# A second scatter table for one token tile, and both tables added when they are loaded

## The chip, the cores and the metric

The kernel runs on one core of one Trainium2 chip. The metric is device microseconds (us) of one execution.

## The reference

One layer of a residual block over 1024 tokens of width 1024: two groups of attention heads, an output projection, and then a PEER channel mixer, which is the part that matters here. For each token, 8 retrieval heads pick 16 of 16384 experts each (product keys of 128 x 128), so a token has 128 experts, each with a gate:

```python
u = expert_down[eb]
act = jax.nn.gelu(jnp.einsum('td,thkd->thk', xb, u), approximate=False) * gb
vv = expert_up[eb]
return jnp.einsum('thk,thkd->td', act, vv)
```

`eb` are the indices of the chosen experts, `gb` their gates. All is float32.

## The kernel before, in words

Tokens lie in eight tiles of 128. Five tiles (block A, tiles 0 to 4) take the dense way through the mixer: every expert is computed for every token, and the activation is multiplied by a gate table, which is zero wherever an expert was not chosen. The three others (block B) take the sparse way: each token's experts are gathered row by row.

The front (to about 1190 us) is the attention, the projections and the routing of both blocks. TensorE, VectorE and ScalarE are fed there by several program streams that a Python merge interleaves (`mrg`), and a planner in the framework sets the order on each queue by priority and its own timing model. The gate tables are made in the front, in two ways:

- Tiles 1 to 4: `gbuild` makes them with one-hot matrices and matmuls, and writes them to the DRAM tensor `gd` (16 DMAs of 2 MB on SP's queue, L1079).
- The one remaining tile (`NSC` is 1): its table `gds[0]` in DRAM, of 128 x 16384 floats (8.4 MB), is first filled with zeros by `zero` (L433 to L438: 16 DMAs of 512 KB from the zero tile `zt`, on SP's queue, pinned in program order, one for each 0.5 of the stream's progress). Then `scatter` (L1028 to L1038) issues 128 indirect DMAs on GpSimd (POOL), one for each of head and choice. Each adds 128 gates, one per token, into the table at computed addresses. A scatter reads and writes the table that the one before wrote, so the framework lets each wait for the landing of the one before.

The indices and gates of the scatters come from `cands` in five groups (L1020 writes the indices). From about 625 us to the end of the front the scatters are all that GpSimd does.

The dense loop (`for gi in range(NG)`, L1368) runs over 32 groups of four chunks; a chunk is 128 experts. The order on TensorE, VectorE and ScalarE is written out by hand there. For each chunk, `split_d` and `split_u` split the weights into a high and a low part (VectorE makes the low part, L1288, L1296), `gelu_s` computes the scores and the GELU (L379 to L381, ScalarE L1304), `mul_g` multiplies by the gates on VectorE (L1310 for the scattered tile, L1312 for the four others), and `split_c` splits the product. After four chunks `up` multiplies by the up weights into ten PSUM banks (L1327 to L1329). `loadg` loads the gates of a group of four chunks: on GpSimd's queue for the first two groups, on SP's queue behind and ahead of the weight loads (L1267, L1269) for the others. `mul_g` of a group's first chunk needs them:

```python
gg, g4 = k.g
c = k.i1 % CG
g3 = k.ge[:, :NSC * P].rearrange("p (s t) -> p s t", t=P)
V.tensor_mul(g3, g3, gg[:, :, c, :])
```

Between the steps of the dense loop, `sp_` (`pump`) issues steps of the sparse way: first the last three `cands` groups of block B, then per expert slot an indirect gather on GpSimd into a ring of five buffers (L1218 for the down rows, L1231 for the up rows) and one VectorE instruction (L1220, L1236).

Of the kernel before, what the change touches and what calls it, by code (L numbers as in the profile page):

```python
# [11 lines left out]
F32 = mybir.dt.float32  # L12
F32R = mybir.dt.float32r
# [4 lines left out]
OP = mybir.AluOpType  # L18
AX = mybir.AxisListType.X

P = 128
# [13 lines left out]
NE = 128  # L35
NSLOT = 128
EPS = 1e-6
BIG = 1e30
# [3 lines left out]
CG = 4  # L42
NG = NE // CG
NPT = 4
NSC = ND - NPT
# [60 lines left out]
def tile_kernel(ctx: ExitStack, tc: tile.TileContext, x, ccol, w_ada, badac, bgt2, gcols, w_in, w_f, bf_, gout,  # L106
                w_out, w_q, keysT, edown, eup, wdense, gfin, out, dbg=None, stop=None):
    nc = tc.nc
    V, S, G, PE = nc.vector, nc.scalar, nc.gpsimd, nc.tensor
    dma = nc.sync.dma_start  # L110
    dbg = dbg or {}

    cst = ctx.enter_context(tc.tile_pool(name="cst", bufs=1))
    dram = ctx.enter_context(tc.tile_pool(name="dram", bufs=1, space=bass.MemoryType.DRAM))

    identf = cst.tile([P, P], F32, name="identf")
    make_identity(nc, identf)
    identr = cst.tile([P, P], F32R, name="identr")
    V.tensor_copy(identr, identf)
    onesf = cst.tile([P, P], F32, name="onesf")  # L120
    V.memset(onesf, 1.0)
    zf = cst.tile([P, 1], F32, name="zf")
    V.memset(zf, 0.0)
    zt = cst.tile([P, P], F32, name="zt")
    V.memset(zt, 0.0)
    mfox = cst.tile([P, P], F32R, name="mfox")
    G.affine_select(mfox, zt, pattern=[[-1, P]], compare_op=OP.is_ge, fill=BIG, base=0, channel_multiplier=1)
    msb = cst.tile([P, P], F32R, name="msb")
    G.affine_select(msb, zt, pattern=[[-1, P]], compare_op=OP.is_gt, fill=-BIG, base=0, channel_multiplier=1)
    iof = cst.tile([P, P], F32, name="iof")  # L130
    G.iota(iof, [[1, P]], base=0, channel_multiplier=0, allow_small_or_imprecise_dtypes=True)
    mhalf = cst.tile([P, 8], F32, name="mhalf")
# [22 lines left out]
    vsp = dram.tile([8, P, T], F32, name="vsp")  # L155
    wsp = dram.tile([24, 2, P, D], F32R, name="wsp")
    gd = dram.tile([NPT * P // SB, P, NE * SB], F32, name="gd")
    gds = [dram.tile([NE * P * P, 1], F32, name="gds%d" % i) for i in range(NSC)]
    pidx = cst.tile([P, 1], F32, name="pidx")
    G.iota(pidx, [[0, 1]], base=0, channel_multiplier=1, allow_small_or_imprecise_dtypes=True)  # L160

# [34 lines left out]
    hpa = ctx.enter_context(tc.tile_pool(name="hpa", bufs=2))  # L196
    hp_[0] = hpa
    wp = front.enter_context(tc.tile_pool(name="wp", bufs=2))
    ps = front.enter_context(tc.tile_pool(name="ps", bufs=2, space=bass.MemoryType.PSUM))
    pin = tc.keep_in_program_order  # L200

# [728 lines left out]
    def cands(blk, gi, v16, i16):  # L930
# [94 lines left out]
            V.tensor_copy(blk.e[:, cols], tm)  # L1025
        yield 1

    def scatter(b, gi):  # L1028
        for k in range(16):
            for r in range(8):  # L1030
                i = (8 * gi + r) % b.nt
                if i < NSC:
                    c_ = (8 * gi + r) * 16 + k
                    off = bass.IndirectOffsetOnAxis(ap=b.e[:, c_:c_ + 1], axis=0)
                    with tc.high_priority(offset=min(0, tc.cur_priority - LOWP)):
                        G.indirect_dma_start(out=gds[i], out_offset=off, in_=b.g[:, c_:c_ + 1], in_offset=None,  # L1036
                                             compute_op=OP.add)
                    yield 1  # L1038

# [134 lines left out]
    def tpool(name, **kw):  # L1174
        return ctx.enter_context(tc.tile_pool(name=name, bufs=2, reuse_waits="tile", **kw))

    dps = tpool("dps", space=bass.MemoryType.PSUM)
    dp0, dpw, dp3, dp2, dp = [tpool(n_) for n_ in ("dp0", "dpw", "dp3", "dp2", "dp")]
# [64 lines left out]
    def pump(n):  # L1243
        while n > 0 and bgs:
            if next(bgs[0], 0) == 0:
                bgs.pop(0)
            else:
                n -= 1
# [23 lines left out]
    def loadg(gi):  # L1272
        i1 = gi * CG
        dma = nc.sync.dma_start if gi > 1 else G.dma_start
        gg = dp.tile([P, NSC, CG, P], F32, name="gg", tag="gg", bufs=2)
        for k in range(NSC):
            dma(gg[:, k], gds[k].rearrange("(p c t) o -> p c (t o)", p=P, t=P)[:, i1:i1 + CG])
        g4 = dp.tile([P, NPT * P // SB, CG, SB], F32, name="g4", tag="g4", bufs=2)
        dma(g4, gd[:, :, i1 * SB:(i1 + CG) * SB].rearrange("s p (c t) -> p s c t", t=SB))
        return gg, g4  # L1280

    def split_d(k, act):
        if act:
            k.dh = dp3.tile([P, D], F32R, name="dh", tag="dh", bufs=2)
            S.activation(k.dh, k.wfd, AF.Copy)
        else:
            k.dl = dp3.tile([P, D], F32R, name="dl", tag="dl", bufs=2)
            V.tensor_sub(k.dl, k.wfd, k.dh.bitcast(F32))  # L1288

    def split_u(k, act):  # L1290
        if act:
            k.uh = dp2.tile([P, D], F32R, name="uh", tag="uh", bufs=UB)
            S.activation(k.uh, k.wfu, AF.Copy)  # L1293
        else:
            k.ul = dp2.tile([P, D], F32R, name="ul", tag="ul", bufs=UB)
            V.tensor_sub(k.ul, k.wfu, k.uh.bitcast(F32))  # L1296

    def gelu_s(k):
        k.ge = dp0.tile([P, TD], F32, name="ge", tag="ge", bufs=2)
        for h in range(2):  # L1300
            cs = slice(h * TH, (h + 1) * TH)
            sp = dps.tile([P, HT], F32, name="sp", tag="sp", bufs=2)
            mm3(sp[:, :TH], k.dh, k.dl, hh, hl, cs)
            S.activation(k.ge[:, cs], sp[:, :TH], AF.Gelu)  # L1304

    def mul_g(k):
        gg, g4 = k.g
        c = k.i1 % CG
        g3 = k.ge[:, :NSC * P].rearrange("p (s t) -> p s t", t=P)
        V.tensor_mul(g3, g3, gg[:, :, c, :])  # L1310
        g3 = k.ge[:, NSC * P:].rearrange("p (s t) -> p s t", t=SB)
        V.tensor_mul(g3, g3, g4[:, :, c, :])  # L1312

    def split_c(k, act):
        if act:
            k.ch = dp2.tile([P, TD], F32R, name="ch", tag="ch", bufs=CG)
            S.activation(k.ch, k.ge, AF.Copy)
        else:
            k.cl = dp2.tile([P, TD], F32R, name="cl", tag="cl", bufs=CG)
            V.tensor_sub(k.cl, k.ge, k.ch.bitcast(F32))  # L1320

    def up(gi, bk, po, k, c):
        tb, dhf = divmod(bk, 2)
        tcs = slice(tb * P, (tb + 1) * P)
        ds_ = slice(dhf * HT, (dhf + 1) * HT)
        per = bk in pers
        PE.matmul(po, k.ch[:, tcs], k.ul[:, ds_], start=c == 0 and (gi == 0 or not per), stop=False)  # L1327
        PE.matmul(po, k.ch[:, tcs], k.uh[:, ds_], start=False, stop=False)  # L1328
        PE.matmul(po, k.cl[:, tcs], k.uh[:, ds_], start=False, stop=c == CG - 1 and (gi == NG - 1 or not per))  # L1329
# [20 lines left out]
    def sp_(n):  # L1350
        pump(n)
# [4 lines left out]
    def nextload():  # L1356
        i1 = next(loads, None)
        if i1 is not None:
            ready.append(load(i1))
# [7 lines left out]
    gcur = loadg(0)  # L1367
    for gi in range(NG):  # L1368
        grp = []
        gnext = loadg(gi + 1) if gi + 1 < NG else None  # L1370
        prev = None
        for c in range(CG + 1):
            cur = nxt if c < CG else None
            if c < CG:
                cur.g = gcur
                grp.append(cur)
            nxt = ready.pop(0) if c < CG and ready else nxt
            if c < CG - 1 and not hasattr(nxt, "dh"):
                split_d(nxt, True)
            if c == CG and gi + 1 < NG:  # L1380
                split_d(nxt, True)
            if cur is not None:
                split_u(cur, True)
            if prev is not None:
                mul_g(prev)
                split_c(prev, True)
            if c < CG - 1 and not hasattr(nxt, "dl"):
                split_d(nxt, False)
            if prev is not None:
                sp_(1)  # L1390
                split_c(prev, False)
            if cur is not None:
                gelu_s(cur)
                split_u(cur, False)
                nextload()
                sp_(PUMP_C - (prev is not None))
            prev = cur
        pos = {}
        for c0, c1 in ((0, CG - 1), (CG - 1, CG)):
            for bk in order[:NPERS]:  # L1400
                for c in range(c0, c1):
                    up(gi, bk, pers[bk], grp[c], c)
        sp_(PUMP_U)
        if gi + 1 == NG:
            pump(10000)
            gf = gfin_tile(dp3, "dh", 2, dma)
            dense_done(order[:NPERS], gf)
        if gi + 1 < NG:
            split_d(nxt, False)
        for n, bk in enumerate(order[NPERS:]):  # L1410
            po = dps.tile([P, HT], F32, name="po", tag="po", bufs=6 - NPERS)
            for c in range(CG):
                up(gi, bk, po, grp[c], c)
            evac(gi, bk, po)
            if gi + 1 < NG and PD and n in (PD, PD + 1) and ready:
                split_d(ready[0], n == PD)
            if gi + 1 == NG:
                dense_done([bk], gf)
            sp_(PUMP_V)
        gcur = gnext  # L1420
# [47 lines left out]
```

## Time and profile before

| | us |
|---|---|
| median of 3 runs (range) | 3099.52 (3094.88 to 3106.32) |
| the profiled execution | 3094.74 |
| its span | 3093.0 |
| TensorE busy in the span | 2871.2 (93%) |
| VectorE busy | 2569.4 (83%) |
| GpSimd busy | 1398.6 (45%) |

The span is the time from the first to the last instruction of the profiled execution; 1.7 us lie around it. Shares of busy time are means over stages with different limits, so the stages are read one by one. Matmuls overlap, so a busy TensorE is not a TensorE at its peak.

### The profile page before, as it was taken

The page shows a single profiled execution, that of the slowest core. Times are in us where ns is not written, and L with a number is a line of the kernel's source. Part 1 is how long each engine was busy: PE and PEld are TensorE (multiplying, and loading weights), DVE is VectorE, ACT ScalarE, POOL GpSimd, SP SyncE. Part 2 cuts the span into 40 slices and gives each one's busy share as a digit, 9 for nine tenths or more (in the row PEclk, how much of TensorE's full clock was granted, in tenths as well). Part 3 has the DMA queues.
Part 4 walks back from the last instruction along what each step waited for, and adds up shares of the span by engine and source line. Part 5 has one row for each costly group of instructions (what it writes and reads, how often), then busy time and mean ns, then how long its engine had stood idle before and what let it go on. Part 6 is the DMA issues. An engine that isn't in the chain of part 4 may idle for free.

```text
span 3093.0 us, 47927 instructions
## 1 busy us (share of the span) xinstructions
PE 2871.2 (93%) x17472; PEld 2657.2 (86%) x17472; DVE 2569.4 (83%) x5250; ACT 1187.6 (38%) x2148; POOL 1398.6 (45%) x962
## 2 busy tenths in 40 slices
PE   5899998998989895489999999999999999999997
PEld 4898998987879895479999899899998988989986
DVE  7676655899997886488889898898898988989996
ACT  5566655446776952132213222122231221322212
POOL 0000000033343423136666776666677656657771
PEclk9999999999999998789999999999999999999998
DMA  7996455655426674359999999999999999999994
GB/s 261 292 305 195 138 224 183 208 172 172 140 45 228 248 260 137 92 206 342 352 339 344 345 336 337 352 351 349 328 343 343 342 331 342 359 328 340 344 331 182
DMA packets 347196, 840.14 MB, mean 272 GB/s; under 512 B 48184, under 2 KB 155728, under 8 KB 344912
## 3 DMA queue, kind: packets, MB, share of 16 engines
q1 hardware_dynamic: 215072, 423.83, 39.9%
q0 software_dynamic: 131888, 413.26, 37.9%
q8 instruction: 137, 2.24, 0.3%
q14 instruction: 99, 0.81, 0.1%
HBM read 734.11 MB, written 102.86 MB: 271 GB/s over the span
## 4 chain that ended last, share of the span: by engine, by line
PE 52%; DVE 22%; DMA 11%; issue 7%; ACT 4%; POOL 3%; SPq 0%; DVEq 0%; POOLq 0%; ACTq 0%
PE sp L379 7%; PE sp L381 6%; PE sp L380 6%; DMA ring<-in_eup,e 5%; PE po L1327 3%; PE po L1328 3%; PE po L1329 3%; DVE sacc L1236 3%; PE pers L1327 2%; PE pers L1328 2%; PE pers L1329 2%; PE proj L379 2%; PE tp L1074 2%; POOL ring L1231 2%; PE proj L380 2%
## 5 line engine op out<-in xcount | busy, mean ns | idle before, releaser
L379 PE MATMUL sp<-hT,dl 128*128 128x320 f32 x2048 | 636.7, 311 | 75.3 <-ACT ge L1304 66.2
L1231 POOL DMA_INDIRECT ring<-in_eup,e x384 | 587.8, 1531 | 249.2 <-DVE sacc L1236 127.7
L1218 POOL DMA_INDIRECT ring<-in_edown,e x384 | 513.5, 1337 | 386.6 <-DVE ring L1220 157.8
L380 PE MATMUL sp<-hT,dh 128*128 128x320 f32 x2048 | 635.9, 311 | 0.0
L381 PE MATMUL sp<-hT,dh 128*128 128x320 f32 x2048 | 635.9, 310 | 0.0
L1236 DVE SCALAR_TENSOR_TENSOR sacc<-ring,sdot,sacc 128x1024 f32<-128x1024 f32 x381 | 488.4, 1282 | 61.9 <-DMA ring<-in_eup,e 56.6
L1220 DVE SCALAR_TENSOR_TENSOR ring<-ring,sx 128x1024 f32<-128x1024 f32 x384 | 461.3, 1219 | 75.5 <-DMA ring<-in_edown,e 73.5
L1036 POOL DMA_INDIRECT gds<-g,e x128 | 247.5, 1933 | 524.1 <-DMA gds<-g,e 370.8
L379 PEld LDWEIGHTS sp<-hT,dl 128*128 128x128 f32 x2048 | 387.5, 189 | 77.4 <-ACT ge L1304 67.6
L1293 ACT ACTIVATE uh<-wfu 128x1024 fp32r<-128x1024 f32 x128 | 134.8, 1053 | 677.6 <-PE po L1329 677.6
L380 PEld LDWEIGHTS sp<-hT,dh 128*128 128x128 f32 x2048 | 387.6, 189 | 1.2
L381 PEld LDWEIGHTS sp<-hT,dh 128*128 128x128 f32 x2048 | 387.3, 189 | 0.0
L1327 PE MATMUL po<-ul,ch 128*128 128x512 f32 x768 | 304.0, 396 | 19.0 <-DVE accB L1336 11.1
L1328 PE MATMUL po<-uh,ch 128*128 128x512 f32 x768 | 301.0, 392 | 0.0
L1329 PE MATMUL po<-uh,cl 128*128 128x512 f32 x768 | 300.6, 391 | 0.0
L1304 ACT ACTIVATE ge<-sp 128x320 f32<-128x320 f32 x256 | 110.6, 433 | 490.6 <-PE sp L381 470.0
L1328 PE MATMUL pers<-uh,ch 128*128 128x512 f32 x512 | 199.6, 390 | 0.0
L1327 PE MATMUL pers<-ul,ch 128*128 128x512 f32 x512 | 199.5, 390 | 0.0
L1329 PE MATMUL pers<-uh,cl 128*128 128x512 f32 x512 | 199.2, 389 | 0.0
L1327 PEld LDWEIGHTS po<-ul,ch 128*128 128x128 f32 x768 | 145.3, 189 | 58.0 <-DVE accB L1336 19.9
L303 POOL TENSOR_TENSOR i<-ms,mhalf 128x4 f32<-128x4 f32 (+1 forms) x16 | 22.1, 1380 | 333.8 <-DVE ms L301 333.8
L1329 PEld LDWEIGHTS po<-uh,cl 128*128 128x128 f32 x768 | 145.3, 189 | 30.9
(306 smaller groups left out, 6469.3 us busy)
## 6 DMA issues: line engine op xcount, KB each, us to landing
wfd<-in_wdense SPq DMA_DIRECT2D x128, 512.0 KB
wfu<-in_wdense SPq DMA_DIRECT2D x128, 512.0 KB
gd<-gt SPq DMA_DIRECT2D x16, 2048.0 KB
g<-gd SPq DMA_DIRECT2D x30, 1024.0 KB
wa<-in_w_ada SPq DMA_DIRECT2D x96, 256.0 KB
wf<-in_w_in SPq DMA_DIRECT2D x48, 512.0 KB
wsp<-wh SPq DMA_DIRECT2D x24, 512.0 KB
wsp<-wl SPq DMA_DIRECT2D x24, 512.0 KB
```

The source lines that it names most:

```text
L379: PE.matmul(pt, wl[:, c], hh[:, kd, cs], start=kd == 0, stop=False)
L380: PE.matmul(pt, wh[:, c], hl[:, kd, cs], start=False, stop=False)
L381: PE.matmul(pt, wh[:, c], hh[:, kd, cs], start=False, stop=kd == KD - 1)
L1036: G.indirect_dma_start(out=gds[i], out_offset=off, in_=b.g[:, c_:c_ + 1], in_offset=None, compute_op=OP.add)
L1218: G.indirect_dma_start(out=r, out_offset=None, in_=edown, in_offset=bass.IndirectOffsetOnAxis(ap=bs.e[:, c_:c_ + 1], axis=0))
L1220: (V.scalar_tensor_tensor(r, r, 1.0, sx, op0=OP.mult, op1=OP.mult, accum_out=s_[:, j:j + 1]))
L1231: G.indirect_dma_start(out=r, out_offset=None, in_=eup, in_offset=bass.IndirectOffsetOnAxis(ap=bs.e[:, c_:c_ + 1], axis=0))
L1236: (V.scalar_tensor_tensor(acc, r, s_[:, j:j + 1], acc, op0=OP.mult, op1=OP.add))
L1293: S.activation(k.uh, k.wfu, AF.Copy)
L1327: PE.matmul(po, k.ch[:, tcs], k.ul[:, ds_], start=c == 0 and (gi == 0 or not per), stop=False)
L1328: PE.matmul(po, k.ch[:, tcs], k.uh[:, ds_], start=False, stop=False)
L1329: PE.matmul(po, k.cl[:, tcs], k.uh[:, ds_], start=False, stop=c == CG - 1 and (gi == NG - 1 or not per))
```

## The change

There are two DRAM tables for the scattered tile instead of one. `zero` fills both (32 DMAs of 512 KB), and the scatters go to the two in turn. `loadg` loads the group's piece of both, the second into a new tile `gg2` with a single buffer, and the first `mul_g` of a group adds the two on VectorE (128 x 512 floats). `loadg` of the next group is no longer issued at the start of a group, but after the `mul_g` of the group's first chunk. To make room for `gg2`, four small constant tiles (`identr`, `zt`, `mfox`, `msb`, 2 KB per partition in all) move into a pool of the front that is freed before the dense loop; the instructions that fill them come later in the program by that.

```diff
-    gds = [dram.tile([NE * P * P, 1], F32, name="gds%d" % i) for i in range(NSC)]
+    gds = [dram.tile([NE * P * P, 1], F32, name="gds%d" % i) for i in range(2)]
...
+    nsct = [0]
...
                 if i < NSC:
+                    nsct[0] ^= 1
...
-                        G.indirect_dma_start(out=gds[i], out_offset=off, in_=b.g[:, c_:c_ + 1], in_offset=None,
+                        G.indirect_dma_start(out=gds[nsct[0]], out_offset=off, in_=b.g[:, c_:c_ + 1], in_offset=None,
                                              compute_op=OP.add)
...
-        gg = dp.tile([P, NSC, CG, P], F32, name="gg", tag="gg", bufs=2)
-        for k in range(NSC):
-            dma(gg[:, k], gds[k].rearrange("(p c t) o -> p c (t o)", p=P, t=P)[:, i1:i1 + CG])
+        gg = dp.tile([P, CG, P], F32, name="gg", tag="gg", bufs=2)
+        g2 = dp.tile([P, CG, P], F32, name="gg2", tag="gg2", bufs=1)
+        for k in range(2):
+            dma((gg, g2)[k], gds[k].rearrange("(p c t) o -> p c (t o)", p=P, t=P)[:, i1:i1 + CG])
...
-        g3 = k.ge[:, :NSC * P].rearrange("p (s t) -> p s t", t=P)
-        V.tensor_mul(g3, g3, gg[:, :, c, :])
+        if c == 0:
+            V.tensor_add(gg, gg, g2)
+        g3 = k.ge[:, :NSC * P]
+        V.tensor_mul(g3, g3, gg[:, c, :])
...
-        gnext = loadg(gi + 1) if gi + 1 < NG else None
+        gnext = None
...
                 mul_g(prev)
+                if c == 1 and gi + 1 < NG:
+                    gnext = loadg(gi + 1)
```

## Rows read from the trace of the kernel before

**Rows 1.** The page's 40 slices: GpSimd (POOL), busy tenths.
```profile
POOL 0000000033343423136666776666677656657771
```

**Rows 2.** Busy us (x instructions) by stretch; clock, DMA share, GB/s.
```profile
core 0: us, PE busy (x) PEld busy (x) DVE busy (x) ACT busy (x) POOL busy (x), PEclk, DMA share, GB/s
...
1206.00:1258.00 52.00, 9.54 (x66) 9.27 (x64) 6.04 (x14) 2.33 (x3) 24.45 (x16) 0.61 0.12 3
1258.00:1320.00 62.00, 38.34 (x186) 34.22 (x187) 42.46 (x160) 18.29 (x26) 4.71 (x6) 0.78 0.40 123
1400.00:2000.00 600.00, 597.87 (x3365) 545.17 (x3364) 535.62 (x703) 151.38 (x221) 394.66 (x279) 1.00 0.96 344
2000.00:2600.00 600.00, 596.21 (x3362) 543.06 (x3362) 535.54 (x704) 152.07 (x223) 393.00 (x279) 1.00 0.95 341
2600.00:2980.00 380.00, 379.90 (x2135) 346.60 (x2134) 341.93 (x429) 93.01 (x136) 258.69 (x177) 1.00 0.96 342
```

**Rows 3.** Timeline of VectorE: start us, us, instruction, [idle <-releaser].
```profile
1211.74 0.57 DVE L999 CAST bq<-cur 128x128 f32<-128x128 bf16 x1
1263.71 0.29 DVE L1310 TENSOR_TENSOR ge<-ge,gg 128x128 f32<-128x128 f32 x1 [51.40 <-DMA gg<-gds]
1269.06 0.69 DVE L1312 TENSOR_TENSOR ge<-ge,g 128x512 f32<-128x512 f32 x1 [5.05 <-DMA g<-gd]
```

**Rows 4.** Timeline of TensorE, same columns.
```profile
1215.23 0.31 PE L381 MATMUL sp<-hT,dh 128*128 128x320 f32 x1
1273.95 0.64 PE L379 MATMUL sp<-hT,dl 128*128 128x320 f32 x1 [58.41 <-ACT ge L1304]
```

**Rows 5.** Timeline of GpSimd: scatters 1, 113, 128, table loads, first gather.
```profile
625.41 1.84 POOL L1036 DMA_INDIRECT gds<-g,e  x1 [138.42 <-DMA wf<-in_w_in]
...
1206.21 1.72 POOL L1036 DMA_INDIRECT gds<-g,e  x1 [4.90 <-DVE bt L986]
...
1257.06 1.55 POOL L1036 DMA_INDIRECT gds<-g,e  x1 [1.77 <-DMA gds<-g,e]
1260.54 0.63 POOL L1277 DMA_DIRECT2D gg<-gds  x1 [1.93 <-DMA gds<-g,e]
1261.35 1.22 POOL L1279 DMA_DIRECT2D g<-gd  x1 [0.18 <-issue]
...
1320.14 1.04 POOL L1218 DMA_INDIRECT ring<-in_edown,e  x1 [55.31 <-DVE cr L960]
```

**Rows 6.** Page's groups, the scatters: busy us, mean ns | idle <-releaser.
```profile
L1036 POOL DMA_INDIRECT gds<-g,e x128 | 247.5, 1933 | 524.1 <-DMA gds<-g,e 370.8
```

**Rows 7.** Timeline of VectorE: indices for scatters 81 to 112, 113 to 128.
```profile
859.10 0.32 DVE L1020 TENSOR_SCALAR e<-tm,pidx 128x128 int32<-128x128 f32 x1
...
918.03 0.29 DVE L1020 TENSOR_SCALAR e<-tm,pidx 128x128 int32<-128x128 f32 x1
```

**Rows 8.** Timeline of GpSimd: one scatter of the late front.
```profile
1025.92 10.63 POOL L1036 DMA_INDIRECT gds<-g,e  x1 [5.88 <-DMA gds<-g,e]
```

**Rows 9.** Stretches as in group 2, with the zero writes and after.
```profile
118.00:184.60 66.60, 64.81 (x475) 63.56 (x473) 48.73 (x100) 41.60 (x99) 3.36 (x3) 1.00 1.02 329
184.60:250.00 65.40, 63.84 (x472) 62.23 (x472) 46.49 (x101) 41.23 (x101) 2.33 (x2) 1.00 0.76 249
```

**Rows 10.** DMA issues: out<-in, queue, count, KB each.
```profile
gds<-zt SPq DMA_DIRECT2D x16, 512.0 KB
...
gg<-gds SPq DMA_DIRECT2D x30, 256.0 KB
```

**Rows 11.** VectorE lines, 1400 to 2980 us: busy, mean ns | idle <-releasers.
```profile
L1312 DVE TENSOR_TENSOR ge<-ge,g 128x512 f32<-128x512 f32 x114 | 78.0, 684 | 22.3 <-ACT ge L1304 22.2
...
L1236 DVE SCALAR_TENSOR_TENSOR sacc<-ring,sdot,sacc 128x1024 f32<-128x1024 f32 x355 | 455.0, 1282 | 59.5 <-DMA ring<-in_eup,e 54.5 <-DVE accB L1336 0.4 <-DVE sacc L1236 0.4
L1220 DVE SCALAR_TENSOR_TENSOR ring<-ring,sx 128x1024 f32<-128x1024 f32 x363 | 436.1, 1219 | 72.8 <-DMA ring<-in_edown,e 70.7 <-DVE accB L1336 0.5
```

**Rows 12.** SP queue's waits, 1400 to 2980 us: total, times, longest.
```profile
SPq L1267 <- DVE dl L1288: 922.5, 107, 18.8
```

More of the change, by code (lines that the diff above doesn't have):

```diff
@@ L117, in tile_kernel @@
     make_identity(nc, identf)
-    identr = cst.tile([P, P], F32R, name="identr")
-    V.tensor_copy(identr, identf)
     onesf = cst.tile([P, P], F32, name="onesf")
@@ L123, in tile_kernel @@
     V.memset(zf, 0.0)
[L124 to L129, printed above, removed]
     iof = cst.tile([P, P], F32, name="iof")
@@ L198, in tile_kernel @@
     wp = front.enter_context(tc.tile_pool(name="wp", bufs=2))
+    identr = wp.tile([P, P], F32R, name="identr", bufs=1)
+    V.tensor_copy(identr, identf)
+    zt = wp.tile([P, P], F32, name="zt", bufs=1)
+    V.memset(zt, 0.0)
+    mfox = wp.tile([P, P], F32R, name="mfox", bufs=1)
+    G.affine_select(mfox, zt, pattern=[[-1, P]], compare_op=OP.is_ge, fill=BIG, base=0, channel_multiplier=1)
+    msb = wp.tile([P, P], F32R, name="msb", bufs=1)
+    G.affine_select(msb, zt, pattern=[[-1, P]], compare_op=OP.is_gt, fill=-BIG, base=0, channel_multiplier=1)
     ps = front.enter_context(tc.tile_pool(name="ps", bufs=2, space=bass.MemoryType.PSUM))
@@ L1274, in loadg @@
         dma = nc.sync.dma_start if gi > 1 else G.dma_start
-        gg = dp.tile([P, NSC, CG, P], F32, name="gg", tag="gg", bufs=2)
-        for k in range(NSC):
-            dma(gg[:, k], gds[k].rearrange("(p c t) o -> p c (t o)", p=P, t=P)[:, i1:i1 + CG])
+        gg = dp.tile([P, CG, P], F32, name="gg", tag="gg", bufs=2)
+        g2 = dp.tile([P, CG, P], F32, name="gg2", tag="gg2", bufs=1)
+        for k in range(2):
+            dma((gg, g2)[k], gds[k].rearrange("(p c t) o -> p c (t o)", p=P, t=P)[:, i1:i1 + CG])
         g4 = dp.tile([P, NPT * P // SB, CG, SB], F32, name="g4", tag="g4", bufs=2)
         dma(g4, gd[:, :, i1 * SB:(i1 + CG) * SB].rearrange("s p (c t) -> p s c t", t=SB))
-        return gg, g4
+        return gg, g4, g2
     def split_d(k, act):
@@ L1306, in mul_g @@
     def mul_g(k):
-        gg, g4 = k.g
+        gg, g4, g2 = k.g
         c = k.i1 % CG
-        g3 = k.ge[:, :NSC * P].rearrange("p (s t) -> p s t", t=P)
-        V.tensor_mul(g3, g3, gg[:, :, c, :])
+        if c == 0:
+            V.tensor_add(gg, gg, g2)
+        g3 = k.ge[:, :NSC * P]
+        V.tensor_mul(g3, g3, gg[:, c, :])
         g3 = k.ge[:, NSC * P:].rearrange("p (s t) -> p s t", t=SB)
```

## The prediction

> **What bounds the kernel now.** I read the page's slices first, then busy time by stretch, then the timelines of the engines around the one stretch in which they stand still, then the groups by line in the dense loop.
>
> GpSimd is about a third busy from the ninth to the sixteenth slice (each is 77 us), almost idle in the seventeenth, and two thirds busy from the nineteenth on [rows 1]. The stretches say what lies at that turn: from 1206 to 1258 us TensorE is busy for 9.5 of 52 us, VectorE for 6.0, the DMA engines for 12%, and only GpSimd works, 24.45 us in 16 instructions [rows 2]. VectorE ends an instruction of the routing at 1212.3 and then sits idle for 51.40 us, until the gate table `gg` has landed, and another 5.05 us until the table of the four other tiles has [rows 3]. TensorE sits idle for 58.41 us behind it [rows 4]. The table load is issued at 1260.54, when the last scatter has landed [rows 5]. So the end of the front waits for the chain of scatters, and nothing else.
>
> The chain: 112 scatters from 625.41 to 1206.21 are 5.19 us apart on average; the last 16, with the chip otherwise quiet, 50.85 / 15 = 3.39 us [rows 5]. A scatter is 1.93 us of GpSimd, and 370.8 us of idle time in all, nearly 3 us for each, are ended by the landing of the scatter before [rows 6]. The last two of the five groups of indices are there at 859 and 918 us [rows 7], so from then on the chain is only working off what has piled up.
>
> The dense loop is bound by TensorE: 597.87 of 600 us, 596.21 of 600, 379.90 of 380 [rows 2]. VectorE (89%) and the DMA engines (96%) are close behind.
>
> **The chain of scatters (removes a wait).** With two tables a scatter waits for the landing of the one before the last. Two are in flight, so the pace is half a round trip, 5.19 / 2 = 2.6 us, unless GpSimd's own 1.93 us, or with a gap some 2.2 us, is more; it is not. The first 80 then end at 625 + 80 x 2.6 = 833 us; the next 32, whose indices come at 859, at 942; the last 16 near 984 us. Bounds for the pace: 1.93 (GpSimd alone) and 5.19 (no gain at all). What matters is one point between them: the chain must end before about 1200 us, which takes (1200 - 625.4) / 128 = 4.49 us, only 13% less than now.
>
> A rule speaks against it. The scatter at 1025.92 took 10.63 us on GpSimd itself, five times the mean [rows 8, 6]. The Trainium skill (SBUF — State Buffer, section "SBUF: two separate sides") says that GpSimd cannot write the descriptors of its DMAs while certain VectorE instructions hold the ports that the two share. By that rule the issue sets the pace where VectorE is dense, a second table takes nothing away, and the time would come out as in rival B below. The trace agrees that it happens, but with a mean of 1.93 us it is rare.
>
> **What the wait gives back.** VectorE can multiply at 1212.3 instead of 1263.71 and 1269.06: 51.40 + 5.05 = 56.45 us. The new addition comes first: 128 x 512 floats, as in the multiply of the same size, 0.68 us [rows 11]. That leaves 55.8 us, if the tables have landed by then. The loads take 1263.71 - 1260.54 = 3.2 us for `gg` and 1269.06 - 1261.35 = 7.7 us for `g4` from issue to use [rows 5, 3]; issued by 1204 they are hidden behind the last of the routing on VectorE. I take them as hidden; bounds 0 and some 18 us (rival A). The first gather of the sparse way comes 56.4 us after the first multiply [rows 3, 5], in VectorE's order, so it moves with it, and the loop after it as a whole. TensorE's granted clock of 0.61 and 0.78 in the stretches around the stall [rows 2] is a mean of its two levels, 1.2 and 2.4 GHz; less of the lower one would be left, but TensorE waits for others there, so I count nothing.
>
> **The second table's zeros (adds).** 16 more DMAs of 512 KB, 8.39 MB [rows 10]. While the first 16 ran, the DMA engines were full, at 329 GB/s, and TensorE was busy for 64.81 of 66.6 us (97.3%); in the stretch after it for 63.84 of 65.4 (97.6%) [rows 9]. The zeros now run on into that stretch, whose DMA share is 0.76. Bounds: 8.39 MB at 329 GB/s in series, 25.5 us, against 0; below 0 only by a luckier order from the planner, which I can't exclude for a few us. The nearest row says 0.3% of 66 us; I take 1 us, which also covers SP's 16 extra issues. If the cover were gone, the loads of the attention on the same queue would come late.
>
> **The second load and the addition in the loop (adds).** Each of 32 groups loads 256 KB more [rows 10]: 8.39 MB, at 344 GB/s [rows 2] 24.4 us of the DMA engines in all. 32 additions of 0.68 us are 21.8 us of VectorE. Upper bound, both in series: 46 us. Lower bound 0: from 1400 to 2980 us VectorE is idle for 1580 - 1413.1 = 166.9 us [rows 2], so there is room for its share, and the DMA share rises by 1.4 points from 0.96. TensorE hides both as long as it is the bound. What leaks through now: 6.0 us of TensorE's idle time for 166.9 of VectorE's; the same ratio of 46 us is 1.7. I take 2 us, and 1 us for the first groups, where VectorE is behind.
>
> **The moved load.** `loadg` now stands after the first multiply of the group before. Its second tile has one buffer, so on SP's queue it waits for the addition, and behind it are the weight loads. These wait for VectorE anyway, 922.5 us in 107 times, for splits that come later in VectorE's order than the addition [rows 12], so they lose nothing. A group is some 55 us, of which about 40 remain for a landing of 7.7. For the second group the load is on GpSimd's queue, ahead of the first gather, which is released much later. Cost 0; the upper bound is one landing of 7.7 us per group where that cover goes, 246 us in 32, which nothing in the rows points to. The constants moved to another pool fill at the start, under the first loads: 0.
>
> **Sum.** 3094.74 (the profiled execution: span 3093.0 and 1.7 around it) - 55.8 + 1 + 2 + 1 = 3042.9 us. The median of the runs is 4.8 us above the profiled one, so 3048 us.
>
> **Rivals.**
> A. The wait shrinks, but a later one takes its place: the tables land late, since their memory comes free only with the last tiles of the front, and the first weights (six panels of 128 x 1024 floats, 3.1 MB, 9.2 us at 341 GB/s) are on the engines at the same time. With both, 9.2 + 7.7 us, about 17 to 18 us of the stall stay: 3066 us. For it: `g4` was the later of the two even on quiet DMA engines [rows 3]. Against it: by the pace above GpSimd would wait with the loads from about 985 us on.
> B. Slower: GpSimd's issue is the pace. Place: the last 48 scatters, which fall in the late front if their issue is held up. Their indices are there from 859 us on [rows 7], so it decides from (1260.5 - 859) / 48 = 8.4 us a scatter; at 9 us the chain ends at 1291, 30 us later than now, and with the 4 us of costs the time is 3134. For it: 10.63 us [rows 8]. Against it: the mean of 1.93, and that idle time ends with a landing [rows 6].
> C. VectorE becomes the bound of the loop through the gathers. It waits 54.5 + 70.7 = 125.2 us for them now [rows 11]; of its 166.9 us of idle time 41.7 remain, less 28 additions (19.1) 22.6. From 18% more waiting, each us costs one. If waits go with the inverse of the free DMA share (0.04 to 0.026) they grow by 54%, 67 us, and 45 are lost: 3093; at 75% it is 3119. For it: the share of 0.96. Against it: TensorE lets so little through now.
> D. The change doesn't do what it says: two scatters in flight take twice as long each. Then the stall stays and the costs come on top: 3104. Against it: the DMA engines are 12% busy in the tail [rows 2], so the wait there is latency.
>
> **How the numbers follow.** A measurement of this kernel can tell about 0.5%, 15.5 us, from no change: 3084 to 3115. Forecast 0.72 and A 0.14 are both faster. C 0.08: half within, a quarter on each side. D 0.03 within. B 0.03 slower. Together faster 0.88, same 0.07, slower 0.05. The range reaches from 3030 (the planner's order of the front luckier by some 10 us and no costs) to 3076 (A, and half of the loop's upper bound, 23 us, without A): it leaves out C, D, B and the ends.
>
> **What would show it.** Right: gaps between scatters halved, the last one before about 1050 us; VectorE's idle time before the first multiply by `gg` under 6 us and TensorE's before its third chunk under 8; the loop's length within 5 us of now. A shows in an idle time of 10 to 20 us there, ended by a table's landing; B in scatters of many us each on GpSimd; C in more than 148 us of waits for `ring` landings in the loop; D in gaps twice as long. Wrong would be a stall that stays over 20 us, or a front that reaches its first dense matmul more than 15 us later.

## The result, and the profile after

1.2% faster: 3063.04 us median (3055.27 to 3071.45) against 3101.95 us for the kernel before on the same chip, ratio 0.9877, 95% interval 0.9844 to 0.9911. The forecast was 3048 us, the range 3030 to 3076. The profiled execution took 3071.45 us, the slowest of its four; its span is 3069.7 us.

The page's slices. GpSimd, to be read against [rows 1]:

```profile
POOL 0000000056756000055666665666666666666661
```

It is half busy or more in five slices (the ninth to the thirteenth) and then idle for four: the scatters are packed closer and end early. Its timeline (start, us, instruction, idle time before and what ended it) answers to [rows 5]:

```profile
993.63 2.03 POOL L1039 DMA_INDIRECT gds<-g,e  x1 [0.30 <-DMA wl<-wsp]
1192.19 1.26 POOL L1281 DMA_DIRECT2D gg<-gds  x2 [196.53 <-DVE cr L960]
1210.99 1.18 POOL L1283 DMA_DIRECT2D g<-gd  x1 [17.54 <-PE sc L381]
...
1291.44 1.04 POOL L1221 DMA_INDIRECT ring<-in_edown,e  x1 [49.19 <-DVE cr L960]
```

The last scatter is at 993.63 us, not at 1257. The load of `gg` then waits 196 us for memory that the routing still holds. The group of scatters, for [rows 6]: the waits for a landing fall from 370.8 to 75.1 us, and a scatter takes no longer.

```profile
L1039 POOL DMA_INDIRECT gds<-g,e x128 | 238.5, 1863 | 263.0 <-DMA wf<-in_w_in 137.5 <-DMA gds<-g,e 75.1 <-issue 26.5
```

VectorE and TensorE at the turn to the dense loop, same columns, for [rows 3, 4]:

```profile
1226.15 1.23 DVE L1292 TENSOR_TENSOR dl<-wfd,dh 128x1024 fp32r<-128x1024 f32 x1 [8.39 <-ACT dh L1289]
...
1240.20 0.68 DVE L1314 TENSOR_TENSOR gg<-gg,gg 128x512 f32<-128x512 f32 x1
1240.99 0.29 DVE L1316 TENSOR_TENSOR ge<-ge,gg 128x128 f32<-128x128 f32 x1
1241.19 0.69 DVE L1318 TENSOR_TENSOR ge<-ge,g 128x512 f32<-128x512 f32 x1
```

```profile
1227.43 0.64 PE L379 MATMUL sp<-hT,dl 128*128 128x320 f32 x1 [15.16 <-DVE dl L1292]
1246.08 0.41 PE L379 MATMUL sp<-hT,dl 128*128 128x320 f32 x1 [1.75 <-ACT ge L1308]
```

The 51.40 and 5.05 us of VectorE and the 58.41 of TensorE are gone. But the first multiply comes at 1240.99 instead of 1263.71, only 22.7 us earlier, and TensorE now waits 15.16 us for the first split of a weight. Busy time by stretch, for [rows 2], shows the old hole filled in part, and a loop that TensorE still bounds:

```profile
core 0: us, PE busy (x) PEld busy (x) DVE busy (x) ACT busy (x) POOL busy (x), PEclk, DMA share, GB/s
1206.00:1258.00 52.00, 34.46 (x192) 33.68 (x191) 36.27 (x121) 18.48 (x25) 3.96 (x5) 0.77 0.57 192
1258.00:1320.00 62.00, 48.52 (x243) 42.20 (x242) 56.80 (x244) 17.40 (x24) 2.41 (x3) 0.90 0.20 60
1400.00:2000.00 600.00, 596.64 (x3336) 541.38 (x3335) 539.11 (x711) 146.47 (x213) 383.51 (x280) 1.00 0.96 345
2000.00:2600.00 600.00, 596.71 (x3315) 538.40 (x3314) 538.11 (x711) 146.75 (x214) 383.85 (x278) 1.00 0.96 346
```

The gathers' groups from 1400 to 2980 us, for [rows 11], wait 61.9 + 62.9 = 124.8 us for landings (125.2 before):

```profile
L1239 DVE SCALAR_TENSOR_TENSOR sacc<-ring,sdot,sacc 128x1024 f32<-128x1024 f32 x364 | 466.4, 1281 | 66.3 <-DMA ring<-in_eup,e 61.9
L1223 DVE SCALAR_TENSOR_TENSOR ring<-ring,sx 128x1024 f32<-128x1024 f32 x351 | 421.0, 1219 | 63.8 <-DMA ring<-in_edown,e 62.9
```

### The profile page after: what moved, and what is told of

It reads as the page before. It is cut to its first block, busy times and chain, and to the rows that moved or that the text cites. A ratio compares the mean times of both kernels' runs of the same rounds, so it can differ in the third digit from the quotient of the medians.

```text
span 3069.7 us, 48010 instructions
## 1 busy us (share of the span) xinstructions
PE 2895.8 (94%) x17472; PEld 2675.8 (87%) x17472; DVE 2588.3 (84%) x5282; ACT 1189.7 (39%) x2148; POOL 1365.3 (44%) x964
## 4 chain that ended last, share of the span: by engine, by line
PE 48%; DVE 22%; DMA 13%; issue 9%; ACT 4%; POOL 4%; SPq 0%; DVEq 0%; POOLq 0%; ACTq 0%
DMA ring<-in_eup,e 7%; PE sp L379 6%; PE sp L381 6%; PE sp L380 6%; DVE sacc L1239 4%; POOL ring L1234 3%; PE po L1333 3%; PE po L1335 3%; PE po L1334 3%; PE tp L1077 2%; PE av L706 2%; DMA wa<-in_w_ada 2%; PE proj L379 2%; PE pers L1333 2%; PE pers L1334 2%
## 5 line engine op out<-in xcount | busy, mean ns | idle before, releaser
L1234 POOL DMA_INDIRECT ring<-in_eup,e x384 | 557.5, 1452 | 289.7 <-DVE sacc L1239 150.3
L1039 POOL DMA_INDIRECT gds<-g,e x128 | 238.5, 1863 | 263.0 <-DMA wf<-in_w_in 137.5
```

What stands on the lines that cost most here:

```text
L1039: G.indirect_dma_start(out=gds[nsct[0]], out_offset=off, in_=b.g[:, c_:c_ + 1], in_offset=None, compute_op=OP.add)
L1234: G.indirect_dma_start(out=r, out_offset=None, in_=eup, in_offset=bass.IndirectOffsetOnAxis(ap=bs.e[:, c_:c_ + 1], axis=0))
```

## The experiments

Theory: the halved chain frees the front; of the stall forecast, part was the luck of one execution, and part comes back as a wait for the first weights. Rivals: the zeros or the planner's order make the front later, or the loop costs more than was booked. Medians are us; ratios are to the kernel before on the same chip. "Front's end" below is the start of the last routing matmul (L877), the chain's end the start of the last scatter.

**The change again, and before again.** No edit.

> The changed kernel once more, unaltered. In its first profile the chain of scatters ended at 996 us as forecast, but the first dense matmul came at 1227 us instead of 1199, so 28 of the 56 us of the stall were given back in the front. Theory (the front is later by its program: 7 us by 430 us, 8 more by 930, 7 more by 1212, 7 more before the first dense matmul): a second profile shows the same marks within 4 us: x1A written back at 482 to 490 us (479 before), last indices of the scatters at 925 to 933 (918 before), first dense matmul at 1223 to 1231 (1199 before); time 3055 to 3072 us. Rival (the profiled execution, the slowest of four, was slow by chance): the first dense matmul comes before 1215 us and the time is under 3058.

> The kernel before once more, unaltered, for a second profile and to see how far two measurements of one kernel lie apart. Theory: ratio within 0.3% of 1; the marks of the front move by up to 5 us from one execution to the next (x1A written back at 476 to 484 us, last routing matmul at 1188 to 1198), the chain of scatters ends within 8 us of 1259, and the dense loop, from the first multiply by the gates to the last, takes 1775 to 1785 us. Rival (the execution profiled before was a lucky one): the last routing matmul comes after 1198 us, which would make the later front of the changed kernel no loss at all.

The change: 3064.86, ratio 0.9885 (0.9847 to 0.9924); its profile has the same wait for `dl` (14.59 us). Before: 3096.7, ratio 1.0003 (0.9981 to 1.0025), profiled at 3089.11. Its front ends at 1205.3 us, where the first profile had 1190.2, but its chain ends at 1253 as there at 1257. VectorE and TensorE of that second profile of before:

```profile
1259.77 0.29 DVE L1310 TENSOR_TENSOR ge<-ge,gg 128x128 f32<-128x128 f32 x1 [34.42 <-DMA gg<-gds]
1265.37 0.69 DVE L1312 TENSOR_TENSOR ge<-ge,g 128x512 f32<-128x512 f32 x1 [5.30 <-DMA g<-gd]
```

```profile
1212.41 0.63 PE L379 MATMUL sp<-hT,dl 128*128 128x320 f32 x1 [6.87 <-DVE dl L1288]
```

The same matmul in the first profile of before:

```profile
1198.86 0.64 PE L379 MATMUL sp<-hT,dl 128*128 128x320 f32 x1 [8.41 <-DVE dl L1288]
```

So the stall of one and the same program was 51.40 us in one execution and 34.42 in another. The chain's end hid how late the front was. Before's second profile meets its rival's mark (a front's end after 1198 us). The change's second profile fits neither side: its first dense matmul is at 1217.39 us. Its front ends at 1202.5 us, that of its first profile at 1212.0; a later front's end by the change itself is not shown.

**One chain.** All scatters go to the first table, all else as in the change.

```diff
-                    nsct[0] ^= 1
+                    pass
```

> As the changed kernel, with both tables zeroed, loaded and added, but every scatter goes to the first table. Theory (the gain is the halved chain and nothing else): the chain ends near 1250 to 1265 us, VectorE waits for the first table until about 1265 to 1275, and the time is 3104 to 3115 us, that is, before plus the costs. Rival for the late front (the denser scatters hold VectorE up between 630 and 930 us): the last indices of the scatters come at 918 to 922 us instead of 929. If they come at 926 or later here too, the denser scatters are not what made that stage longer. Rival for the gain (the gain comes from the moved load or from another order, not from the chain): the time stays below 3085.

3084.06, ratio 0.9959 (0.9941 to 0.9976). The scatters end at 1249.4 us, and the wait is back:

```profile
1256.81 0.69 DVE L1314 TENSOR_TENSOR gg<-gg,gg 128x512 f32<-128x512 f32 x1 [15.06 <-DMA gg<-gds]
```

The turns alone are worth 19 to 21 us (3084.06 against 3064.86 and 3063.04). The theory missed: it had 3104 to 3115 us, and the time is just below the 3085 us set for the rival, by which another order brings the gain. So the chain is about half of it; the next run shows the other half. The execution profiled, at 3099.59 us, is the slowest of ten, 15 us above their median.

**The second table's zeros alone**, on the kernel before, with the table unused:

```diff
-... for i in range(NSC)]
+... for i in range(2)]
```

> The kernel before with one part of the change alone: a second table is filled with zeros and never used. Theory (the zeros change the planned order of TensorE in the front, and that costs 12 to 15 us up to the last routing matmul, little of it by 430 us): last routing matmul at 1202 to 1206 us instead of 1190, but the time stays within 5 us of before, since the chain of scatters is what ends last and covers it. Rival 1 (the zeros cost nothing, the lateness is that of the alternating scatters): last routing matmul at 1187 to 1194. Rival 2 (the zeros hold up the whole front, chain included): the chain ends over 10 us later and the time is over 3108.

3079.61, ratio 0.9938 (0.9913 to 0.9964): 19 us faster than before, with more work. The expectation, within 5 us of before, missed. The planner orders the front otherwise (its end is at 1208.8 us), and the chain ends earlier, at 1247.0 us:

```profile
1253.49 0.29 DVE L1310 TENSOR_TENSOR ge<-ge,gg 128x128 f32<-128x128 f32 x1 [23.75 <-DMA gg<-gds]
```

By the starts on GpSimd's timeline, scatters 65 to 97 take 198.2, 185.6 and 196.8 us in the three profiles with the order of before (e7 below is the third), and 170.0 and 171.0 in e5 and e4. In that stretch (917 to 1115 us in the first profile) VectorE makes one-hot tiles, and single scatters hang: they stand on GpSimd for many us. GpSimd and VectorE in the first profile of before, beside the 10.63 us of [rows 8]:

```profile
1049.30 13.59 POOL L1036 DMA_INDIRECT gds<-g,e  x1 [5.87 <-DMA gds<-g,e]
```

```profile
1060.25 1.22 DVE L1070 TENSOR_TENSOR o<-ob,gT 128x1024 f32<-128x1024 bf16 x1
1061.65 1.29 DVE L1057 TENSOR_TENSOR ob<-io,ib 128x1024 bf16<-128x1024 bf16 x2 [0.17 <-ACT o L1066]
```

The scatter ends at 1062.89, 1.4 us after VectorE's first pause in it, one of 0.17 us; until then VectorE's instructions follow each other without one. The second profile of before has the same: 13.75 us, ended 1.4 us after a pause of 0.17. In e5 another order stands there, and the longest scatter takes 5.97 us:

```profile
1066.53 5.97 POOL L1036 DMA_INDIRECT gds<-g,e  x1 [5.85 <-DMA gds<-g,e]
```

The two long ones, 24.2 us, against 5.97 are most of the 28 us by which the stretch is shorter than in the first profile. That the rest is also order, and not chance, is not shown. And much of it is lost again behind: scatters 97 to 128 take 164.8 and 164.6 us in e5 and e4, 141.9, 151.6 and 141.8 in the three others. In all, e5's chain ends 6 to 20 us before theirs, 2 to 9 of them by an earlier start. So the added zeros bring the gain, by all signs through the order; that it comes mainly from the scatters that no longer hang is not shown.

**The constants alone** on the kernel before:

```diff
-    identr = cst.tile([P, P], F32R, name="identr")
...
+    identr = wp.tile([P, P], F32R, name="identr", bufs=1)
```

> The kernel before with one part of the change alone: the four small constants are in the front's pool wp and not in the pool that stays. Nothing else; TensorE's instructions stand in the order of before. My theory: that move shifts the tiles of the dense loop by 2 KB per partition, so the first weights land on memory that the routing still uses: the first dl comes 12 to 16 us after the last routing matmul (before and its repetition: 7.4 and 5.9), and costs nothing in time here, since the chain of scatters ends later than both: within 6 us of the kernel before (ratio 0.998 to 1.002), the first multiply by gg 6 to 7 us after the last scatter as before. Rival: the shift comes from gg2 or from the moved load; then the distance stays at 6 to 8 us here.

3095.43, ratio 0.9989 (0.9971 to 1.0007): as expected no change in time, but the wait for the first weights is there, and it is the load's wait on SP's queue for a routing tile (waits from 1170 to 1235 us: total, times, longest):

```profile
1220.37 0.64 PE L379 MATMUL sp<-hT,dl 128*128 128x320 f32 x1 [13.74 <-DVE dl L1288]
```

```profile
SPq L1267 <- DVE i L890: 21.8, 1, 21.8
```

In the change the same wait is 21.7 us, in the first profile of before 7.6, for a later load. The first weight load is issued 12.7 us before the front's end there, here 7.8 behind it, when the last top-k (L890) is done. So shifted by 2 KB, the first weight tile lies on memory that this top-k still writes. Here the chain covers that; in the change nothing does.

**`gg2` in another pool**: it is taken from the loop's first pool, so that the tiles behind keep their places.

```diff
-        g2 = dp.tile([P, CG, P], F32, name="gg2", tag="gg2", bufs=1)
+        g2 = dp0.tile([P, CG, P], F32, name="gg2", tag="gg2", bufs=1)
```

> The tile gg2 is taken in the first of the dense pools instead of the last, which moves the weight tiles of the dense loop back by 2 KB to where they lay before; the planned order of every engine stays the same but for a few lines. Theory (the first weight load waits for a routing tile whose memory it got when the constants moved): the first weight load is issued 12 us before the last routing matmul as before, near 1200 us, not 6 us after it at 1217.8; the first dense matmul follows the last routing matmul by 8 to 9 us, not 15; the time falls by 6 to 7 us, to about 3056. Rival (VectorE's routing is the bound there, whatever the weights do): the gap stays at 15 us and the time at 3063.

> The kernel of e2 once more, with nothing changed, beside e10 on the same chip, to see whether its gain over the change stands: 3056 us, 3052 to 3062, ratio 0.986 to 0.988. The rival: its 8.6 us over the unaltered change were the chip or the executions drawn; then it gives 3062 to 3066, as the change and its repetition.

3056.22, ratio 0.9868 (0.9833 to 0.9903), and again 3055.27, 0.9873 (0.9839 to 0.9907): by the medians 7 to 10 us below the change. TensorE's wait is back to what it was:

```profile
1210.17 0.64 PE L379 MATMUL sp<-hT,dl 128*128 128x320 f32 x1 [7.61 <-DVE dl L1292]
```

Now the table is the last to land, but only just: VectorE's addition waits 0.39 us for it, and 0.89 in the repetition. This is the fastest of the versions that leave nothing out; its interval overlaps the change's, so the gain over it rests on two pairs of medians and the wait that went.

**Zeros elsewhere in the order.** First the stream with the zeros is made slower by its weight, then the second table's zeros become a stream of their own in later stages (on top of e2):

```diff
-ZR2 = 23.1
+ZR2 = 12.0
```

> The zero writes of both tables are spread over about twice the time (their weight in the merge is 12.0 instead of 23.1), so the DMA engines, full from 118 to 250 us in the changed kernel, have room for the attention's own loads. Theory (the zeros cost the first attention 7 us): x1A is written back near 479 to 482 us instead of 486, and the time falls by 3 to 7 us, to 3056 to 3060. Rival (TensorE does not feel the zeros; the 7 us are another order from the planner): the mark stays at 484 or later, or moves either way by some us without relation to the DMA share.

```diff
-    zr = zgen[0] = zero()
+    zr, zr2 = zero(gds[:1]), zero(gds[1:])
+    zgen[0] = chain(zr, zr2)
...
-    ..., bg=((pp, PP3), (zr, ZR3)))
+    ..., bg=((pp, PP3), (zr2, 12.0)))
```

> As the kernel with gg2 in the first dense pool, but the second table's zeros are a stream of their own in the stages after the first attention, so the planner makes another order for the whole front. Theory (what the front loses is the order that the planner happens to make): the last routing matmul moves by 3 us or more from the 1202 us of the kernel that it is compared with, either way, and the time with it, 3045 to 3065. Rival (the loss comes from the DMA engines being full while the first attention runs): the mark of x1A and the last routing matmul both move earlier by 3 to 12 us, and the time falls below 3052.

3073.98 (0.9922; 0.9894 to 0.9951) and 3071.43 (0.9915; 0.9891 to 0.9939): 9 and 15 us slower than what they were made from, and both behind the 3056 to 3060 and 3045 to 3065 that had been expected. In the first, the wait for the first weights grew (20.1 us from the last routing matmul to VectorE's first `dl`, 14.2 in the change); in the second all of the front is later (its last index at 946 us, not 923). The place given to the zeros early is no loss; their own cost is not separated from the order.

**One load.** Of the change, the second load and the addition are taken away.

```diff
-        g2 = dp.tile([P, CG, P], F32, name="gg2", tag="gg2", bufs=1)
-        for k in range(2):
+        g2 = None
+        for k in range(1):
...
-        if c == 0:
-            V.tensor_add(gg, gg, g2)
```

> The changed kernel without the second table's load and without the addition (the gates of every second scatter are left out of the result); the scatters still alternate. Theory (the load and the addition cost the dense loop 5 to 8 us): from the first multiply by the gates to the last 1775 to 1779 us instead of 1780 to 1788, and TensorE's idle time from 1400 to 2900 us back to 6 us from 8 to 14; time 3056 to 3060 beside 3064. Rival (VectorE's and the DMA engines' room hides both): the loop stays at 1780 to 1788 us and the time at 3064.

3054.35, ratio 0.9852 (0.9809 to 0.9895): 9 to 11 us for load and addition by the medians, where the theory had 5 to 8. From the first multiply by `gg` to the end its profile has 1822.0 us; the change and its repetition 1828.7 and 1836.4, before 1829.3 and 1827.5, the last two with 5.05 and 5.30 us of VectorE's wait for `g4` in them [rows 3].

**Merge once.** Both tables, but the second is added to the first in DRAM by 16 DMAs that add at their target, so the loop loads one; the constants stay. Then the same with the DMAs in pairs behind the gate-table writes.

```diff
+        if gi == 4:
+            for q in range(NE * P * P // (P * D)):
+                v = [g_.rearrange("(q p f) o -> q p (f o)", p=P, f=D)[q] for g_ in gds]
...
+                    G.dma_start(out=v[0], in_=v[1], accum_op=OP.add, max_dma_last_dim=4096)
```

> The kernel before with both tables and the scatters in turn, as in the change, but the second table is added to the first once in DRAM: 16 DMAs of 512 KB that add at their target, issued on GpSimd behind the last scatter. So the loop loads one table and adds nothing, gg2 is not needed, and the constants stay where they were before. My theory: the scatters end near 985 us; GpSimd is idle from there to 1190 us and the DMA engines are 0.60 to 0.68 busy in that stretch, so the merge (25 MB read and written, some 75 us at 340 GB/s) fits there. Then the first dl comes 6 to 8 us after the last routing matmul, as in e2, and the loop from the first to the last multiply by gg takes about 1776 us, as in before and e6, and not 1780 to 1790: 3046 us, 3040 to 3054, below e2 (3056.2). Rival 1: the adding DMAs are slow (one after the other, each for the landing of the one before, or with small elements): over 13 us each the merge ends behind 1200 us and the stall is back in part, or they hold up the gd writes and the front ends over 10 us later: 3060 to 3090. Rival 2: the planner's new order of the front decides; then the last routing matmul leaves 1202 to 1212 us, where it was in the kernels with both tables, by more than 5 us.

```diff
+            mk = gp.tile([P, 1], F32, name="mk", bufs=1)
+            G.tensor_copy(mk, gt[:, 0, 0:1])
+        for _ in range(min(2, 16 - nmer[1])):
...
+            pin(G.dma_start(out=v[0], in_=v[1], accum_op=OP.add, max_dma_last_dim=4096))
```

> As e9 (both tables, the second added to the first in DRAM, one load in the loop, constants as before), but the 16 adding DMAs are spread: two behind each of eight writes of the gate tables of the other tiles, the third to the tenth, each pair held by a one-column copy on GpSimd that reads what is written. In e9 all 16 ran from 995 to about 1065 us; the DMA engines were full from 990 to 1070, and TensorE was busy for 58.2 of these 80 us against 71.4 in e2: 13 us, about what the front was late. My theory: that was the cost of e9, so spread over some 120 us the merge costs less than half of it; the last routing matmul is back at 1202 to 1212 us, the loop is as in e9 (1822 us from the first multiply by gg to the end), and the time is 3048 us, 3040 to 3056. Rival 1: GpSimd's issue is held up by VectorE's one-hot instructions, which run back to back in this stretch (in before two scatters took 10.63 and 13.59 us there, and ended when VectorE first paused for 0.1 us or more); then adding DMAs of over 5 us each show, the merge ends behind 1200 us and the time is 3060 to 3085. Rival 2: the planner's order costs what it did in e9 whatever the merge does: 3060 to 3070 with a front as late as in e9 (last routing matmul 1217).

3065.86 (0.9896; 0.9873 to 0.9918) and 3061.19 (0.9891; 0.986 to 0.9922): neither beats e2, and both miss their theories (3040 to 3054 and 3040 to 3056). The loop is short as in e6 (1821.9 and 1824.8 us), and the wait for the first `dl`, with the constants in their old place, is 5.94 and 6.62 us. But the front ends at 1217.5 and 1218.6. The stretch with the merge, in e9 and then in e2:

```profile
990.00:1070.00 80.00, 58.20 (x380) 54.44 (x379) 45.43 (x73) 44.96 (x78) 13.92 (x17) 0.85 1.02 290
```

```profile
990.00:1070.00 80.00, 71.37 (x510) 66.50 (x510) 60.27 (x94) 60.82 (x111) 0.00 (x0) 0.96 0.55 215
```

While the DMA engines are full TensorE does 13.2 us less. Most of it can be seen as a wait: VectorE may overwrite `x1B` only when its write to DRAM has landed, and TensorE waits for VectorE (e9, waits from 985 to 1060 us: total, times, longest):

```profile
DVE x1B L453 <- DMA x1d<-x1B: 13.4, 2, 10.2
PE proj L473 <- DVE x1B L453: 9.5, 2, 8.0
```

In e2 neither wait is there, which points to the merge for a part of e9's late front. In e10 they are 4.4 and 2.8 us; six of the pairs' DMAs still went at once (their writes were done), TensorE had 65.78 us in the stretch, and the front was late all the same. So pacing was tried only by half, and whether the merge or the planner's order makes e10 late is open. One of its one-column copies on GpSimd hung like the scatters above, until VectorE's first pause:

```profile
1064.87 10.18 POOL L1053 COPY mk<-gt 128x1 f32<-128x1 f32 x1 [15.74 <-ACT gt L1096]
```

```profile
1075.26 1.29 DVE L1076 TENSOR_TENSOR ob<-io,ib 128x1024 bf16<-128x1024 bf16 x2 [0.25 <-ACT o L1085]
```

## Why the prediction was right, and where it was off

- **The chain: right.** Forecast 2.6 us a scatter and an end near 984; measured 362 / 127 = 2.85 (a wait of 20 us for indices included) and 993.6, 991.0 and 979.2 in the change, its repetition and e2.
- **What the wait gives back, 55.8 us: right in kind, too large.** The term was read from one execution whose front ended early. The two profiles of before have 51.40 and 34.42 us; their mean, 42.9, with the other 5.2 and less the addition, gives 47.4. The stretch was read rightly, but the term is a difference between two ends, and only the chain's showed in the time; so the front's was never seen to vary. It does: 1190.2, 1205.3 and 1206.4 us in three profiles of that order. Once the chain is gone, the front's end is the bound, and with it what stands behind it; the first multiply came 22.7 us earlier, not 55.8.
- **The constants, booked at 0: wrong.** Their move alone (e7) puts the weight tiles onto late memory; `gg2`, taken behind the weights, has no part in it, and taken ahead of them it takes the shift back (e2). It costs some 7 us (TensorE waits 15.16 and 14.59 for the first `dl`, 8.41 and 6.87 in before, 7.61 in e2), and 7 to 10 by the medians. Rival A, a later wait in the old one's place, had the right kind of cause and named the tables; the weights' own memory was what came late. One test set for "wrong", a first dense matmul more than 15 us later, is met by it: the first that reads `dl` comes at 1227.43, and at 1198.86 and 1212.41 in the two profiles of before.
- **The zeros, booked at 1 with a few us of luck below: the luck was mis-sized.** The new order alone gave 19 us while the chain was the bound (e5), and the turns gave 19 to 21 more against e4, which has the second table's zeros and all the other added work. So half of the gain, as the runs take it apart, came with an order that was not forecast. Had the turns come first, they might have given nearly all of it, since with two tables the last scatter is before 1020 us in every run; two tables in the old order were not run.
- **The loop, booked at 3: too small.** From the first multiply to the end before has 1829.3 and 1827.5 us, but 5.05 and 5.30 of them are the wait for `g4`, which the forecast had already counted in the stall. Without it they are 1824.2 and 1822.2, as in e6, e9 and e10 with one load (1821.9 to 1824.8); the change and its repetition have 1828.7 and 1836.4. So the second load and the addition cost 9.3 us on average, as they do by the medians of e6: TensorE does not hide them as nearly as the ratio of idle times had it.
- **The moved load at 0: nothing against it.** e6 has the new place, e9 the old one, and both loops are 1822 us.
- **The sum.** Forecast 51.8 us less; measured 38.9 by the medians (33.0 in the repetition), but only 23.3 between the profiled executions. Between the means of the two profiles each, 3091.9 and 3070.3 us, the terms add up: 47.4 of stall, less 9.5 for a later front's end (1197.7 and 1207.3), 7.3 for the first weights (from the front's end to the first dense matmul) and 9.3 for the loop, give 21.3; measured 21.6. But both profiles of before lie below their medians, those of the change above. So some 11 to 17 us of the gain lie in executions that no profile shows, and that the median fell within the range is in part luck.
- **The rivals.** B: scatters do get held up beside VectorE, for 10.63, 13.59 and 13.75 us in before, but the mean is 1.86 us after the change, whose last scatter comes before that stretch. The Trainium skill (SBUF — State Buffer, section "Who interferes with whom") has the loser blocked for the whole of one VectorE instruction, and a tensor_tensor in the way of GpSimd's reads alone; here over ten tensor_tensors of 0.6 to 1.2 us went by in a row during the scatter of 13.59 us, so the trace agrees that GpSimd is blocked and differs on for how long. That VectorE is the cause is read from the times at which five such instructions ended; no run tested it. C: the gathers wait 124.8 us against 125.2. D: the waits for landings fell to a fifth.

## What to carry to other kernels

A wait's length in one profile is the distance between two ends, and the earlier one is invisible in the time: price its removal from several executions. A tile put into or out of a pool moves all tiles behind it, so ask of the first loads of the next stage whose memory they now wait for. And where a planner orders the work, run the added work without its use as a control: here that alone moved the time by 19 us. Measure a stage from a mark behind every wait that another term has counted: 5 us of a wait at the stage's start hid half of what the loop's additions cost.

## What the runs showed of the hardware

A GpSimd instruction, be it an indirect DMA or a one-column copy, can stand for over 10 us while VectorE runs 128x1024 one-hot instructions back to back. The four scatters of 10.63 to 13.75 us in the profiles with the order of before ended 1.4 us after a pause of VectorE of 0.10 to 0.17 us had begun, the copy of 10.18 us in e10 as one of 0.25 us began. This is read from the timelines; no run tested it. Closer scatters were not longer: the first 64 take 1.86 us on average in before, at 4.6 us from one to the next, and 1.79 in the change, at 2.7 us. While sixteen DMAs of 512 KB that add in DRAM ran in e9 beside the front's other transfers, the DMA engines were full for much of 80 us at 290 GB/s, less than the 344 of the loop's plain loads and gathers.
